# Modulation blocks queued behind feed-forward steps, and tap products and softmax division on ScalarE, in a two-block Trainium2 kernel

## The chip, the cores and the metric

The kernel runs on one core of a Trainium2 chip. The metric is device time in microseconds (us). The engines are TensorE (PE; PEld is its weight load), VectorE (DVE), ScalarE (ACT), GpSimd (POOL) and SyncE (SP), whose queue issues the DMAs. Each engine executes its instructions in the order in which the program has them; what a wait holds up, holds up all that is behind it on that engine.

## What is computed

Two transformer blocks, one behind the other, on 256 tokens of 1024 channels in fp32. The first is feed forward, mixer, feed forward, norm. The second has two layers, each a feed forward, a mixer and a feed forward, and carries a second stream, a context of 256 tokens (C, beside the tokens' X). Its norms are modulated by vectors that are computed from a condition:

```python
mod = jax.nn.silu(c) @ w_ada[l] + b_ada[l]          # 9 vectors of 1024 a layer; c_ctx likewise
sh1, sc1, gt1, sh2, sc2, gt2, sh3, sc3, gt3 = jnp.split(mod, N_ADA, axis=-1)
h = h + HALF * gt1 * swiglu_2(ada_norm(h, g_ffn1[l], sh1, sc1), w1_ffn1[l], w3_ffn1[l], w2_ffn1[l])
...
# in the mixer: convolution module, attention, Fourier branch
v = a * jax.nn.sigmoid(gt)
v = lax.conv_general_dilated(v, w_dw[:, None, :], ...)   # 31 taps on each of 384 channels
p = jax.nn.softmax(s, axis=-1)
o = jnp.einsum('bhqk,bkhd->bqhd', p, v)
```

## The kernel before

**Products.** Every fp32 product is made of three. A weight block `wr` of 512 KB is loaded, `split` casts it to a high part `wh` on ACT (L94) and subtracts that on DVE for the low part `wl` (L95); `mm3` (L110) then issues high by high, high by low and low by high. Activations are split the same way (`gH`, `gL`, `xH`, `xL`, `r`). There are 3 buffers each of `wr`, `wh` and `wl`, and in PSUM 3 of `pg` and 2 of `pm`.

**Feed forwards.** `ffn` (L210) runs over 22 blocks of 128 hidden channels in groups of 8, 7 and 7. For each block of a group comes a gating step (two weight blocks, 48 products, then `sl`, `gg` and the split of `gg`); behind a group come 8 down steps (one weight block, 24 or 21 products, and a `residual` into `h`, L292). The two feed forwards of the first block work on 256 columns (called FFN1a and FFN1b here); those of the second block work on both streams, 512 columns (a[0], b[0], a[1]), apart from the last.

**Modulation.** `ada(l, i)` (L340) computes the three vectors of one feed forward or mixer: 24 blocks, each one DMA of 512 KB into `wa` (2 buffers) and for each stream a multiply-and-sum over `wa` on DVE into `wz` (L356, 1 buffer). `ada(0,0)` runs in FFN1a, `ada(0,1)` and `ada(0,2)` are issued at a[0], `ada(1,0)` at b[0], and `ada(1,1)` and `ada(1,2)` behind it for a[1]. What orders all instructions is a scheduler: each has a priority, by the order of the code, and `spread_over` (L335) gives the blocks of `ada` priorities spread evenly over a stretch, so that they are taken when an engine has room.

**Norms and hand-over.** `norm_streams` (L295) norms a stream into `xH`, `xL`. For the first feed forward of the second block the context's norm stands ahead of FFN1b in the code; `hand_over` (L784) ends the first block and norms X. a[0] starts with three gating steps split by stream (`lead`), the context first.

**Mixers.** A `Mixer` is made for each stream and layer: mc and mx in layer 0, and mx in layer 1 (there mc gives keys and values alone). `conv_in` writes the 384 gated channels, in three tiles of 128, with padding to `vpad`. `taps` (L1158 on) sums the 31 taps of two tiles on DVE (L1164). `taps_pool` (L1149 on) does the third tile on POOL: for taps 1 to 30 a product into `tap`, 1 buffer (L1155), and an addition to the sum (L1156). Next on PE come keys (`ktc`, `ktx`), values (`vc`, `vx`), queries (`w_uq`, four blocks of 768 columns; copies to `qT`, L1074) and `attention`: scores, exp on ACT (L1101), the division by a multiply with 1/`den` on DVE (L1103), transposes (L1106) and products with the values.

## Time and profile before

| | us |
|---|---|
| median of 3 runs (2726.71 to 2731.24) | 2728.09 |
| profiled execution, its own time | 2729.1 |
| its span | 2727.3 |
| PE busy | 2622.9 (96%) |
| DVE busy | 1938.3 (71%) |
| ACT busy | 1153.4 (42%) |
| POOL busy | 334.0 (12%) |

The span is one execution on the chip as the profiler recorded it; the time of the profiled execution is 1.8 us longer than its span and 1.0 us above the median. An engine's busy time counts its own instructions. Rows of a timeline give the start in us, the duration, engine, line, operation, output and inputs; "x3" means three instructions in a row, and the brackets at the end give how long the engine stood idle before and what ended that. Matmul durations overlap, so the pace of PE is read from starts, not durations. PEclk is the clock that TensorE was granted, 1.00 for 2.4 GHz.

### The profile page before, as it was taken

Reading aid. Unit: us, or ns where it says so; the run is one execution under the profiler, and the core shown is the slowest. Engines: PE = TensorE matmul, PEld = TensorE weight load, DVE = VectorE, ACT = ScalarE, POOL = GpSimd, SP = SyncE. Lnnn points to the kernel's source line nnn. Section 1 sums busy time; section 2 is a strip of 40 time slices with the busy share of each in tenths; the row PEclk is TensorE's granted clock in tenths of the full one; section 3 lists DMA queues with packets and bytes.
Section 4 is the critical chain, followed back from the end, with each engine's and each line's share of the span. In section 5 each row is a group of like instructions: output and inputs, shape, how many; then the busy total and the mean of one; then the engine's idle time right before and its main releaser. Section 6 shows DMA issues by size and latency. Waiting matters only on the chain.

```text
span 2727.3 us, 44461 instructions
## 1 busy us (share of the span) xinstructions
PE 2622.9 (96%) x17394; PEld 2372.5 (87%) x17394; DVE 1938.3 (71%) x3490; ACT 1153.4 (42%) x1940; POOL 334.0 (12%) x354
## 2 busy tenths in 40 slices
PE   7999999998999999998999999999999999899998
PEld 7998979998788888788899878789888889799998
DVE  8988877668996359859877998736333348967666
ACT  5445535444222236654565322224222236566444
POOL 1110311110000006507300000000000002800000
PEclk9999999999999999999999999999999999999999
DMA  7774404655674234234556677733232333246564
GB/s 266 255 224 150 148 23 150 182 174 188 219 226 142 95 94 142 84 96 135 171 155 195 223 225 232 246 103 98 87 95 90 101 108 113 74 140 194 179 184 133
DMA packets 129770, 418.47 MB, mean 153 GB/s; under 512 B 18159, under 2 KB 25839, under 8 KB 129176
## 3 DMA queue, kind: packets, MB, share of 16 engines
q1 hardware_dynamic: 129160, 415.23, 48.8%
q8 instruction: 137, 2.24, 0.3%
q14 instruction: 73, 0.60, 0.1%
q10 hardware_dynamic: 400, 0.39, 0.0%
HBM read 414.24 MB, written 1.33 MB: 152 GB/s over the span
## 4 chain that ended last, share of the span: by engine, by line
PE 67%; DVE 18%; issue 7%; DMA 5%; ACT 2%; POOL 0%; DVEq 0%; SPq 0%; ACTq 0%; POOLq 0%
PE pg L113 15%; PE pg L112 15%; PE pg L114 15%; PE pm L112 6%; PE pm L113 6%; PE pm L114 6%; DVE wl L95 5%; DMA wa<-in_w_ada 4%; DVE wz L356 3%; DVE f L1164 3%; ACT wh L94 1%; PE pa L1113 1%; PE pm L1096 1%; PE pt L1106 1%; DVE un L180 1%
## 5 line engine op out<-in xcount | busy, mean ns | idle before, releaser
L94 ACT CAST wh<-wr 128x1024 fp32r<-128x1024 f32 (+3 forms) x664 | 649.8, 980 | 1108.3 <-PE pg L113 687.7
L95 DVE TENSOR_TENSOR wl<-wr,wh 128x1024 fp32r<-128x1024 f32 (+3 forms) x664 | 760.9, 1147 | 330.6 <-ACT wh L94 325.0
L114 PE MATMUL pg<-xH,wl 128*128 128x256 f32 (+2 forms) x2176 | 674.0, 310 | 7.8 <-DVE wl L95 7.8
L112 PE MATMUL pg<-xH,wh 128*128 128x256 f32 (+2 forms) x2176 | 672.4, 310 | 7.3 <-ACT wh L94 6.1
L113 PE MATMUL pg<-xL,wh 128*128 128x256 f32 (+2 forms) x2176 | 672.2, 309 | 0.5 <-DVE xL L199 0.5
L114 PEld LDWEIGHTS pg<-xH,wl 128*128 128x128 f32 x2176 | 413.4, 190 | 32.9 <-DVE wl L95 9.9
L112 PEld LDWEIGHTS pg<-xH,wh 128*128 128x128 f32 x2176 | 413.2, 190 | 31.1 <-ACT wh L94 6.1
L113 PEld LDWEIGHTS pg<-xL,wh 128*128 128x128 f32 x2176 | 413.1, 190 | 24.2 <-issue 2.2
L112 PE MATMUL pm<-xH,wh 128*128 128x256 f32 (+2 forms) x1112 | 366.4, 330 | 5.8 <-ACT wh L94 4.2
L114 PE MATMUL pm<-xH,wl 128*128 128x256 f32 (+2 forms) x1112 | 365.9, 329 | 0.8 <-DVE wl L95 0.8
L113 PE MATMUL pm<-xL,wh 128*128 128x256 f32 (+2 forms) x1112 | 366.5, 330 | 0.0
L356 DVE CUSTOM_DVE_ANT_0 wz<-wa,cb,vec 128x1024 f32<-128x1024 f32 x256 | 332.7, 1300 | 42.9 <-DMA wa<-in_w_ada 39.6
L112 PE MATMUL pg<-gH,wh 128*128 128x256 f32 (+1 forms) x972 | 325.3, 336 | 10.7 <-ACT gH L94 9.7
L113 PE MATMUL pg<-gL,wh 128*128 128x256 f32 (+1 forms) x972 | 326.0, 336 | 1.7 <-DVE gL L95 1.5
L114 PE MATMUL pg<-gH,wl 128*128 128x256 f32 (+1 forms) x972 | 324.8, 335 | 1.2 <-DVE wl L95 1.2
L112 PEld LDWEIGHTS pm<-xH,wh 128*128 128x128 f32 x1112 | 210.2, 189 | 27.2 <-ACT wh L94 4.4
L114 PEld LDWEIGHTS pm<-xH,wl 128*128 128x128 f32 x1112 | 210.3, 189 | 22.0 <-DVE wl L95 1.3
L113 PEld LDWEIGHTS pm<-xL,wh 128*128 128x128 f32 x1112 | 210.2, 189 | 20.4
L112 PEld LDWEIGHTS pg<-gH,wh 128*128 128x128 f32 x972 | 183.8, 190 | 33.1 <-ACT gH L94 11.7
L113 PEld LDWEIGHTS pg<-gL,wh 128*128 128x128 f32 x972 | 184.3, 190 | 24.3 <-DVE gL L95 3.9
L114 PEld LDWEIGHTS pg<-gH,wl 128*128 128x128 f32 x972 | 184.0, 189 | 21.9 <-DVE wl L95 1.6
L112 PE MATMUL pg<-r,wh 128*128 128x256 f32 x560 | 161.2, 288 | 8.4 <-DVE qT L1076 4.5
(408 smaller groups left out, 3658.8 us busy)
## 6 DMA issues: line engine op xcount, KB each, us to landing
wa<-in_w_ada SPq DMA_DIRECT2D x144, 512.0 KB, 4.3
wr<-in_w13a SPq DMA_DIRECT2D x88, 512.0 KB, 3.6
wr<-in_w13b SPq DMA_DIRECT2D x88, 512.0 KB, 4.1
wr<-in_w_bg SPq DMA_DIRECT2D x72, 512.0 KB, 3.5
wr<-in_w_in SPq DMA_DIRECT2D x67, 512.0 KB, 3.6
wr<-in_w_1b SPq DMA_DIRECT2D x52, 512.0 KB, 3.9
wr<-in_w_1a SPq DMA_DIRECT2D x51, 512.0 KB, 4.5
wr<-in_w_out SPq DMA_DIRECT2D x32, 512.0 KB, 4.4
```

The lines of the kernel that those rows point to most:

```text
L94: self.nc.scalar.copy(H, src)
L95: self.nc.vector.tensor_tensor(L, src, H.bitcast(F32), op=ALU.subtract)
L112: mm(ps, aH, bH, start=start, stop=False)
L113: mm(ps, aH, bL, start=False, stop=False)
L114: mm(ps, aL, bH, start=False, stop=stop)
L180: nc.vector.scalar_tensor_tensor(u, src[:, k, s], gain[:, k:k + 1], y, op0=ALU.mult, op1=ALU.mult)
L356: nc.vector.tensor_tensor_reduce(z, w, self.cb[:, s], 1.0, self.v("b_ada", l)[:, c:c + 1], ALU.mult, ALU.add, self.cols[l][:, c, s:s + 1])
L1096: mm(ss[:, n * T:(n + 1) * T], self.qT[:, h, _blk(t)], kt[:, h], start=True, stop=True)
L1106: nc.tensor.transpose(pt[:, _blk(n)], E[:, _blk(n)], net.ident)
L1113: mm(po[64 * e:64 * e + 64, _blk(t)], keys[n // 2][1][:, n % 2, 64 * h:64 * h + 64], ets[e][:, _blk(n)], start=n == 0, stop=n == nk // P - 1)
L1164: nc.vector.scalar_tensor_tensor(acc[:, j], self.pads[:, j, t:t + T], self.w31[:, j, t:t + 1], acc[:, j], op0=ALU.mult, op1=ALU.add)
```

## The change

Four things change.

1. `ada` no longer issues its blocks. It queues them, and a new `drip` takes blocks from the queue behind each of the first 38 gating and down steps of a feed forward: as many as are left, divided by the steps that are left of the 38, rounded up. Of 24 queued blocks one goes behind each of the first 24 steps, of 12 one behind each of the first 12, of 48 two behind each of the first 10 and one behind each of the next 28. Each `wz` is ordered behind the last DVE instruction of its step (`issue_after`). `spread_over` is gone.
2. `ada(0,0)` is cut in two: 12 blocks in FFN1a, 12 in FFN1b, for which the condition's rows are loaded (`ada_rows`) once more. `ada(1,1)` and `ada(1,2)` are in a[1] and no longer in b[0] as well.
3. The context's norm for a[0] stands behind FFN1b, since the blocks that it needs now end in it.
4. In the mixers the tap products go from POOL to ACT, with 2 buffers of `tap`; the additions stay on POOL. The softmax's multiply by 1/`den` goes from DVE to ACT.

```diff
     def split(self, H, L, src):
         self.nc.scalar.copy(H, src)
-        self.nc.vector.tensor_tensor(L, src, H.bitcast(F32), op=ALU.subtract)
+        return self.nc.vector.tensor_tensor(L, src, H.bitcast(F32), op=ALU.subtract)
...
+        slots = MF + 3 * KD - 8
...
+            def drip(ins):
+                nonlocal slots
+                if slots > 0:
+                    self.drip(ins, slots)
+                slots -= 1
...
-                gating(m, p)
+                drip(gating(m, p))
...
-                down(m, W, self.pg(), s)
+                drip(down(m, W, self.pg(), s))
...
-    def ada(self, l, i, pool, pace, streams=(0, 1)):
+    def ada(self, l, i, pool, streams=(0, 1), part=range(24)):
...
+        def block(j, after):
             c = 24 * i + j
-            tc.cur_priority = pace.pop(0)
             w = self.sb(pool, [P, D], "wa", 2)
             nc.sync.dma_start(w, self.A["w_ada"][l, c])
             for s in streams:
...
                 z = self.sb(pool, [P, D], "wz", 1)
+                with self.tc.issue_after(after.ins):
+                    nc.vector.tensor_tensor_reduce(z, w, self.cb[:, s], 1.0, self.v("b_ada", l)[:, c:c + 1],
+                                                   ALU.mult, ALU.add, self.cols[l][:, c, s:s + 1])
+            if j == 23:
+                self.ada_end(l, i, streams)
+
+        self.queue += [lambda after, j=j: block(j, after) for j in part]
+
+    def drip(self, ins, left):
+
+        for _ in range(-(-len(self.queue) // left)):
+            self.queue.pop(0)(ins)
...
-                    self.ada(0, 0, fp, self.spread_over(24, 150, 1500))
+                    self.ada(0, 0, fp, part=range(12))
...
-                self.norm_streams(C, m[0][0], m[0][1])
                 xn, (self.xH, self.xL) = (self.xH, self.xL), x1
                 with pool("ff") as fp:
+                    self.ada_rows(fp)
+                    self.ada(0, 0, fp, part=range(12, 24))
                     self.ffn(A["w13_1b"], A["w2_1b"], X, 0.5, r, fp=fp)
             self.xH, self.xL = xn
+            self.norm_streams(C, m[0][0], m[0][1])
...
-                p = self.spread_over(48, 350, 1400)
-                self.ada(0, 1, fp, p[:24])
-                self.ada(0, 2, fp, p[24:])
+                self.ada(0, 1, fp)
+                self.ada(0, 2, fp)
...
-                self.ada(1, 0, fp, self.spread_over(24, 150, 1200))
+                self.ada(1, 0, fp)
...
-                p = self.spread_over(48, 150, 1200)
-                self.ada(1, 1, fp, p[:24])
-                self.ada(1, 2, fp, p[24:], (0,))
+                self.ada(1, 1, fp)
+                self.ada(1, 2, fp, (0,))
...
-                    nc.vector.tensor_scalar(E, E, den, None, op0=ALU.mult)
+                    nc.scalar.activation(E, E, AF.Copy, scale=den)
...
-            z = self.sb([P, T], "tap")
-            nc.gpsimd.tensor_scalar(z, self.pads[:, 2, t:t + T], self.w31[:, 2, t:t + 1], None, op0=ALU.mult)
+            z = self.sb([P, T], "tap", 2)
+            nc.scalar.activation(z, self.pads[:, 2, t:t + T], AF.Copy, scale=self.w31[:, 2, t:t + 1])
             nc.gpsimd.tensor_tensor(acc[:, 2], acc[:, 2], z, op=ALU.add)
```

The order of instructions changes in three places that matter here. First ACT in layer 0, from the values of the context's mixer to its first exp. A name's numbers tell its buffer; 768 columns are a block of `w_uq`, 1024 columns a block of the next projection, `w_in` of mx. Before:

```order
L1062 COPY vc_1795_10526<-pg_1922_11160 128x512
L94 CAST wh_1935_11231<-wr_1934_11229 128x768
L1074 COPY qT_1923_11168<-pg_1927_11175 64x256
L94 CAST wh_1940_11261<-wr_1939_11259 128x768
L1074 COPY qT_1923_11168<-pg_1928_11187 64x256
L1074 COPY qT_1923_11168<-pg_1932_11205 64x256
L94 CAST wh_2052_11586<-wr_2051_11584 128x1024
L1074 COPY qT_1923_11168<-pg_1933_11217 64x256
L1074 COPY qT_1923_11168<-pg_1937_11235 64x256
L94 CAST wh_2056_11618<-wr_2055_11616 128x1024
```

After, the end of the same stretch (the first tap stands 31 rows ahead of the first row here; from there on two taps stand between one other instruction and the next):

```order
L1164 ACTIVATE tap_1903_11072<-vpad_1850_10800,w31_1849_10798 128x256
L94 CAST wh_1931_11204<-wr_1930_11202 128x768
L1164 ACTIVATE tap_1904_11075<-vpad_1850_10800,w31_1849_10798 128x256
L1164 ACTIVATE tap_1905_11078<-vpad_1850_10800,w31_1849_10798 128x256
L94 CAST wh_1936_11234<-wr_1935_11232 128x768
L1164 ACTIVATE tap_1906_11081<-vpad_1850_10800,w31_1849_10798 128x256
L1164 ACTIVATE tap_1907_11084<-vpad_1850_10800,w31_1849_10798 128x256
L1083 COPY qT_1924_11171<-pg_1933_11208 64x256
```

And at its end:

```order
L1164 ACTIVATE tap_1911_11096<-vpad_1850_10800,w31_1849_10798 128x256
L1083 COPY qT_1924_11171<-pg_1938_11238 64x256
L94 CAST wh_1941_11264<-wr_1940_11262 128x768
L1083 COPY qT_1924_11171<-pg_1939_11250 64x256
L1110 ACT_TABLE_LOAD
L1110 ACTIVATE f2_1951_11301,den2_1950_11298<-pm_1948_11295,mx2_1949_11297 128x256
L94 CAST wh_2053_11589<-wr_2052_11587 128x1024
```

The 30 taps now stand among the casts of `w_uq`: the second of its four casts stands behind tap 22, the third behind tap 24, the last behind tap 30, and the first cast for `w_in` moved from ahead of the exp to behind it.

Second, DVE at the first down steps of FFN1a. Before, at the last down steps of its first group:

```order
L292 SCALAR_TENSOR_TENSOR h_1_69<-pg_203_1036,h_1_69 128x256
L356 ISA wz_56_224,mod0_24_161<-wa_54_220,cb_26_163,vec_2_70 128x1024
L356 ISA mod0_24_161 128x1
L95 TENSOR_TENSOR wl_216_1131<-wr_214_1128,wh_215_1130 128x1024
L292 SCALAR_TENSOR_TENSOR h_1_69<-pg_207_1068,h_1_69 128x256
```

After:

```order
L299 SCALAR_TENSOR_TENSOR h_1_69<-pg_133_776,h_1_69 128x256
L358 ISA wz_129_768,mod0_24_161<-wa_127_764,cb_26_163,vec_2_70 128x1024
L358 ISA mod0_24_161 128x1
L95 TENSOR_TENSOR wl_146_849<-wr_144_846,wh_145_848 128x1024
L358 ISA wz_135_804,mod0_24_161<-wa_134_802,cb_26_163,vec_2_70 128x1024
L358 ISA mod0_24_161 128x1
L299 SCALAR_TENSOR_TENSOR h_1_69<-pg_140_814,h_1_69 128x256
```

Where a down step had one `wz`, each of the first four has two; behind the twelfth step there is none. FFN1b, which had none, has the same pattern.

Third, DVE in b[0], at the last gating step of its second group. Before:

```order
L356 ISA wz_3506_19608,mod1_25_162<-wa_3505_19606,cb_2984_16665,vec_2_70 128x1024
L356 ISA mod1_25_162 128x1
L356 ISA wz_3508_19612,mod1_25_162<-wa_3507_19610,cb_2984_16665,vec_2_70 128x1024
L356 ISA mod1_25_162 128x1
L247 TENSOR_TENSOR gg_3244_18244<-sl_3243_18242,pm_3242_18217 128x512
```

After:

```order
L248 TENSOR_TENSOR gg_3237_18231<-sl_3236_18229,pm_3235_18204 128x512
L95 TENSOR_TENSOR wl_3256_18314<-wr_3254_18311,wh_3255_18313 128x896
L95 TENSOR_TENSOR gL_3149_17722<-gg_3237_18231,gH_3148_17721 128x512
L358 ISA wz_3239_18237,mod1_25_162<-wa_3238_18235,cb_2985_16668,vec_2_70 128x1024
L358 ISA mod1_25_162 128x1
```

Before, `gg` stood behind two `wz`; after, the `wz` stand behind the step's `gg` and `gL`.

## Rows read from the trace of the kernel before

**Rows 1.** Stage windows: length, then PE, PEld, DVE, ACT, POOL busy (instructions), clock, DMA:

```profile
0.00:205.00 205.00, 186.41 (x1508) 183.33 (x1509) 179.86 (x283) 95.25 (x137) 30.34 (x32) 0.98 0.76 249
...
461.00:630.00 169.00, 166.67 (x1398) 165.47 (x1399) 110.35 (x161) 78.60 (x114) 26.00 (x18) 1.00 0.60 180
...
1046.00:1156.00 110.00, 100.48 (x715) 88.04 (x714) 102.06 (x223) 68.06 (x165) 74.15 (x75) 0.98 0.34 104
...
1224.00:1360.00 136.00, 120.17 (x958) 117.04 (x958) 120.99 (x198) 64.88 (x109) 74.69 (x67) 0.97 0.51 156
...
2250.00:2380.00 130.00, 117.42 (x856) 108.37 (x855) 114.85 (x247) 74.13 (x156) 70.76 (x80) 0.95 0.31 98
```

**Rows 2.** Timeline of POOL in layer 0, from the first tap:

```profile
1060.08 1.08 POOL L1155 TENSOR_SCALAR tap<-vpad,w 128x256 f32<-128x256 f32 x1
1061.24 0.74 POOL L1156 TENSOR_TENSOR f<-f,tap 128x256 f32<-128x256 f32 x1
1062.09 1.77 POOL L1155 TENSOR_SCALAR tap<-vpad,w 128x256 f32<-128x256 f32 x1
...
1075.41 1.54 POOL L1156 TENSOR_TENSOR f<-f,tap 128x256 f32<-128x256 f32 x1
```

**Rows 3.** Groups of POOL by line (count, busy us, mean ns, idle us before):

```profile
L1155 POOL TENSOR_SCALAR tap<-vpad,w 128x256 f32<-128x256 f32 x90 | 106.2, 1180 | 8.6
L1156 POOL TENSOR_TENSOR f<-f,tap 128x256 f32<-128x256 f32 x90 | 83.2, 924 | 7.5
```

**Rows 4.** Timeline of ACT in layer 0, beside those taps:

```profile
1064.53 0.83 ACT L94 CAST wh<-wr 128x768 fp32r<-128x768 f32 x1 [0.42 <-PE pg L113]
...
1081.83 0.42 ACT L132 ACTIVATE acc<-fb 128x256 f32<-128x256 f32 x1
```

**Rows 5.** Timeline of PE there, at two blocks of queries:

```profile
1068.29 0.58 PE L112 MATMUL pg<-r,wh 128*128 128x256 f32 x1 [2.62 <-DVE qT L1078]
...
1073.48 0.47 PE L112 MATMUL pg<-r,wh 128*128 128x256 f32 x1
```

**Rows 6.** Timeline of POOL in layer 1, its first tap:

```profile
2320.21 1.08 POOL L1155 TENSOR_SCALAR tap<-vpad,w 128x256 f32<-128x256 f32 x1
```

**Rows 7.** Timeline of PE in layer 1, at two blocks of queries:

```profile
2331.92 0.58 PE L112 MATMUL pg<-r,wh 128*128 128x256 f32 x1 [4.53 <-DVE qT L1076]
...
2337.59 0.28 PE L114 MATMUL pg<-r,wl 128*128 128x256 f32 x1
```

**Rows 8.** Line L1103: count, min/median/max in ns, and who waited for it:

```profile
L1103 DVE TENSOR_SCALAR f<-f,den x48: 396/488/953, 1078.5 to 2399.6; 128x512 f32<-128x512 f32 x32, 128x256 f32<-128x256 f32 x16
...
  PE pt L1106: 5.1, 13
```

**Rows 9.** Timeline of DVE in FFN1a, one down step and its modulation block:

```profile
139.38 1.09 DVE L95 TENSOR_TENSOR wl<-wr,wh 128x896 fp32r<-128x896 f32 x1
140.39 0.42 DVE L292 SCALAR_TENSOR_TENSOR h<-pg,h 128x256 f32<-128x256 f32 x1
140.72 1.28 DVE L356 CUSTOM_DVE_ANT_0 wz<-wa,cb,vec 128x1024 f32<-128x1024 f32 x1
...
141.93 1.09 DVE L95 TENSOR_TENSOR wl<-wr,wh 128x896 fp32r<-128x896 f32 x1
```

**Rows 10.** Timeline of DVE in FFN1b, two residuals of following down steps:

```profile
552.79 0.42 DVE L292 SCALAR_TENSOR_TENSOR h<-pg,h 128x256 f32<-128x256 f32 x1 [0.35 <-PE pg L114]
...
555.25 0.42 DVE L292 SCALAR_TENSOR_TENSOR h<-pg,h 128x256 f32<-128x256 f32 x1 [0.47 <-PE pg L114]
```

**Rows 11.** Timeline of PE at three of its longest waits:

```profile
137.03 0.50 PE L112 MATMUL pg<-gH,wh 128*128 128x256 f32 x2 [2.88 <-ACT gH L94]
...
656.42 0.98 PE L163 MATMUL pn<-io,hy 128*128 128x128 f32 x3 [6.76 <-DVE hy L798]
...
1725.24 0.79 PE L112 MATMUL pg<-gH,wh 128*128 128x512 f32 x1 [4.65 <-ACT gH L94]
```

**Rows 12.** Window behind the third of them (columns as in rows 1):

```profile
1723.00:1730.00 7.00, 4.60 (x10) 3.32 (x11) 5.97 (x11) 1.56 (x2) 0.00 (x0) 0.51 0.78 235
```

More of the change, by code (lines that the diff above doesn't have):

```diff
@@ L247, in gating @@
                     nc.vector.tensor_tensor(gg, sl, p[1][:, :w], op=ALU.mult)
-                self.split(gH[:, m], gL[:, m], gg)
+                return self.split(gH[:, m], gL[:, m], gg)
+            def drip(ins):
[3 more added lines that the diff above has]
+                slots -= 1
             nl = 3 if lead and gi == 0 else 0
@@ L257, in ffn @@
                 for m in range(nl):
-                    gating(m, pss[2 * m:2 * m + 2])
+                    drip(gating(m, pss[2 * m:2 * m + 2]))
             for m in range(nl, n):
@@ L271, in down @@
                              k == 0, k == n - 1)
-                self.residual(m, ps[:, rel(q)], q, gate)
+                return self.residual(m, ps[:, rel(q)], q, gate)
             nt = 4 if tail and gi == len(GROUPS) - 1 else 0
@@ L291, in residual @@
             sc = gate if isinstance(gate, float) else gate[:, m, q.start // T:q.start // T + 1]
-            self.nc.vector.scalar_tensor_tensor(self.h[:, m, q], src, sc, self.h[:, m, q],
-                                                op0=ALU.mult, op1=ALU.add)
+            r = self.nc.vector.scalar_tensor_tensor(self.h[:, m, q], src, sc, self.h[:, m, q],
+                                                    op0=ALU.mult, op1=ALU.add)
+        return r
     def norm_streams(self, s, gain, shift):
@@ L333, in ada_rows @@
         self.nc.scalar.activation(self.cb, self.cb, AF.Silu)
-    def spread_over(self, n, start, length):
-        p = self.tc.cur_priority
-        return [p + start + length * i // n for i in range(n)]
-    def ada(self, l, i, pool, pace, streams=(0, 1)):
-        nc, tc = self.nc, self.tc
-        prio = tc.cur_priority
-        for j in range(24):
+    def ada(self, l, i, pool, streams=(0, 1), part=range(24)):
+        nc = self.nc
+        def block(j, after):
             c = 24 * i + j
-            tc.cur_priority = pace.pop(0)
             w = self.sb(pool, [P, D], "wa", 2)
@@ L355, in ada @@
                 z = self.sb(pool, [P, D], "wz", 1)
-                nc.vector.tensor_tensor_reduce(z, w, self.cb[:, s], 1.0, self.v("b_ada", l)[:, c:c + 1],
-                                               ALU.mult, ALU.add, self.cols[l][:, c, s:s + 1])
-        tc.cur_priority = prio
-        self.ada_end(l, i, streams)
+                with self.tc.issue_after(after.ins):
[7 more added lines that the diff above has]
+            self.queue.pop(0)(ins)
     def ada_end(self, l, i, streams):
@@ L850, in build @@
                 with pool("ff") as fp:
-                    self.mod = [{}, {}]
+                    self.mod, self.queue = [{}, {}], []
                     self.cols = [self.sb(self.cp, [P, 72, 2], f"mod{l}") for l in range(2)]
                     self.ada_rows(fp)
-                    self.ada(0, 0, fp, self.spread_over(24, 150, 1500))
+                    self.ada(0, 0, fp, part=range(12))
                     self.ffn(A["w13_1a"], A["w2_1a"], X, 0.5, r, fp=fp, first=first)
```

## The prediction

> **What bounds the kernel now.** I read the stage table first [rows 1]: for each stretch, its length, PE's busy time, DVE's, and the clock. PE fills 166.7 of 169 us in FFN1b and 186.4 of 205 in FFN1a; what it loses, it loses in few places, above all the three mixer stretches: 110 − 100.5 = 9.5 us, 136 − 120.2 = 15.8 and 130 − 117.4 = 12.6. In these DVE is busy 102, 121 and 115 us, that is some 90% of the time: there DVE sets the pace, and POOL's 74 us (tap products and additions, [rows 3]) lie beside it. So PE is the bound nearly everywhere, and a saving on DVE or POOL counts only where PE stands idle today. Second come the single waits of PE [rows 5, 7, 11], which name what ended them. Third, the order of the instructions on ACT: ACT is busy 68 of 110 us in the first mixer stretch, so there is room for 30 more instructions, but what decides is what stands behind them.
>
> **Taps on ACT, the largest term.** Removed: 90 products on POOL, 106.2 us [rows 3]. Nobody waits for them today; the additions' result is wanted only at the end of the convolution. Added: 90 products on ACT. Such an instruction isn't in the trace; the nearest is a 128x256 ACT pass from memory to memory, 0.42 us [rows 4], and 30 of them make 12.6 us a mixer. That time isn't the price. The price is a wait: with two `tap` buffers, tap t+2 waits for addition t on POOL, and ACT goes no further until then. The 30 taps stand in the middle of the casts for `w_uq`, so the casts take the pace of POOL's additions. The last `w_uq` cast stands behind tap 30, and tap 30 behind addition 28.
>
> Pace of an addition: the shortest is 0.74 us [rows 2], from its start to the next instruction's 0.85; by the mean of 0.924 [rows 3] it is about 1.02; one that falls beside a weight split on DVE took 1.54 [rows 2]. I take 0.92, between the two, since few weight splits run in a stretch in which the casts are held. 28 additions: 25.8 us, with ends of 23.8 and 28.6.
>
> The Trainium skill, "GPSIMD Engine Reference", section Key points, says that GpSimd shares its SBUF interfaces with VectorE and contends with DVE instructions that have two SBUF inputs, which the 1.54 us addition agrees with. Its section on elementwise cycle accounting gives a two-input operation about 2.6 cycles an element at 1.2 GHz; an estimate from that page for 256 elements is 0.55 us and some fixed cost, and at 0.55 the two large mixer terms would be 28 × 0.37, some 10 us, smaller each. It makes the two-input operation the dear one, while here the one-input products' mean of 1.18 us is above the additions' 0.924 [rows 3], and the measurement decides.
>
> Layer 0, the context's mixer: the first tap starts at 1060.1 [rows 2], so tap 30 ends at 1060.1 + 0.4 + 25.8 + 0.4 = 1086.7. Behind it a copy (about 0.4, like the pass), the last `w_uq` cast (0.83, [rows 4]) and its `wl` (about 0.9, from 1.01 for 896 columns [rows 9]): its products start at about 1088.8. Today they start at 1073.48 [rows 5]. That is 15.3 us later, and PE has nothing else, since every weight block behind it (the `w_in` of the other mixer) needs a cast that stands further back on ACT. The wait of 2.62 us [rows 5] is inside this. PE comes out of so long a wait at half clock: in b[0], behind one of 4.65 us that ends at 1725.24 [rows 11], the granted clock is 0.51, the lower level of 1.2 GHz, up to about 1730 [rows 12], and 4.8 us at half speed lose 2.4. I take +2. DVE goes on with its own taps meanwhile, so the stretch behind, which has its share of the 9.5 us that PE idles [rows 1], may give back 3 to 4. Net 15.3 + 2 − 4, +13 (10 to 17).
>
> Layer 1: first tap at 2320.2 [rows 6], tap 30 ends at 2346.8, the last block's products start 2.1 us later, at 2348.9. Today they start at about 2338: PE stood still until 2331.92 for a query copy on DVE, and is through the third block at 2337.59 [rows 7]. 11 us later, +2 for the clock, −2 given back: +11 (8 to 14).
>
> Layer 0, the tokens' mixer (from 1247): the same 30 taps, but DVE is busy without a break there and casts have more slack, so ACT's delay of 2 to 7 us lies mostly beside DVE's, and POOL has left the stretch some 40 us sooner: +1 (−4 to +6).
>
> **The softmax division.** 48 multiplies leave DVE, 0.49 us each at the median [rows 8], 24 us, and come to ACT at some 0.4 to 0.6. PE waited 5.1 us for them in 13 places [rows 8]; it will now wait for ACT, behind a cast at worst: 0 (−3 to +3).
>
> **FFN1a.** A block is two `wz`; from start to start one takes 1.21 us, a `wl` of 896 columns 1.01 and a residual 0.33 [rows 9]; a `wl` of 1024 columns, in proportion, 1.15. A down step takes PE 2.46 us with 21 products [rows 10], so 2.81 with the 24 of the first group. With one `wz` a step DVE needs 1.15 + 0.33 + 1.21 = 2.69 and keeps up. With a whole block it needs 3.90, 1.09 more than PE. Four such steps: +4.4, the lower end being what the three weight buffers let DVE run ahead, some 2 us. Today's wait of 2.88 us at the end of the second group's gating [rows 11] goes, as its blocks are now in FFN1b. Gating steps are balanced: two `wl`, two `wz` and three small ones like the residual, 5.7 us, against 48 products, 5.6. I take +2 (0 to +4).
>
> **FFN1b.** It has no block today and idles 2.3 us in all [rows 1]. The same four steps cost +4.4, and at the end of the group's gating `gg` queues behind a block, as it did where PE waited 2.88 us [rows 11]; I take 1.6 of that. +6 (+3 to +9).
>
> **Hand-over.** Today 8 `wz` stand in the short chain of small instructions that makes the norm's factor, and PE waits 6.76 us [rows 11]. These go. But the context's norm, which ran inside FFN1b, now starts when FFN1b ends, and PE has no product until its factor is there: a chain of the same kind, with nothing to hide it. One such wait in place of another: 0. The nearest row gives both ends: −7 if only the old wait goes, +7 if a second one comes beside it.
>
> **a[0]**: four `wz` behind a gating step make DVE's step 2.3 + 4.8 + some 1.2 us = 8.3 against PE's 11.2 (twice the 5.6, with twice the columns), and the later down steps are as today: +0.5. **b[0]**: today `gg` stands behind two `wz`, PE waits 4.65 us [rows 11], and the half clock behind it loses 2.4 more. After, no block stands ahead of `gg` there: −7 (−8 to −4). a[1] gets blocks that DVE has room for: 0.
>
> **Sum.** +13 + 11 + 1 + 0 + 2 + 6 + 0 + 0.5 − 7 = +26.5 us on the profiled 2729.1, so 2755.6; that execution lies 1.0 above the median, so against the median 2728.1 + 26.5 = 2754.6. I put 2754.
>
> **The rivals.**
> A, faster: ACT isn't held. This decides at one number: between two pairs of taps ACT has one copy of 0.37 us and the two taps, together some 1.1 us; if an addition comes in under 0.55 us, POOL is never late. Against it: the shortest takes 0.74, and 0.85 to the next start [rows 2]. For it: POOL loses over half of its 189 us on taps [rows 3], so DVE meets it less often. Then the mixers win instead of losing: of the 37.9 us that PE idles there, I give a third to a half, −15; with FFN1a, FFN1b, a[0] and b[0] at +1.5 it ends at 2728.1 − 13.5 = 2714.6. Chance 0.13. A weaker form of it, in which the order on PE lets most of the wait be given back behind, because DVE is then far ahead (mixers +6): 2728.1 + 6 + 1.5 = 2735.6, between 2725 and 2740; chance 0.15.
>
> B, much slower: additions at 1.02 us, nothing given back, the hand-over with a second wait and FFN1b at its upper end: mixers +37 (17 + 14 + 6), the rest +1.5 + 7 + 3: 2728.1 + 48.5 = 2776.6. Chance 0.15. What would set it off is that DVE, with its backlog of own taps, keeps slowing POOL.
>
> C, the change doesn't do what it says: the scheduler could have put the blocks elsewhere. The order shows each `wz` behind its step, so I give it no chance of its own.
>
> **Numbers.** The forecast has 0.57, from 2740 to 2766; A's two forms 0.28; B 0.15. The range leaves out a part of A's first form and the tip of B: 2714 to 2778. A difference of 0.2%, 5.5 us, is about what a measurement of this kernel can tell from none. Faster by more than that is A's first form and a small part of its second: 0.16. Within it, most of the second: 0.10. Slower: 0.74.
>
> **What would show it.** Right: in the profile after, ACT's taps in layer 0 spread over some 26 us, each second one waiting for an addition on POOL; PE idle for over 10 us between 1060 and 1090 and again near layer 1's taps, ended by a `w_uq` cast or its `wl`; no wait of 4 us in b[0]; waits of about 1 us at each of the first down steps of FFN1b, ended by `wl`; a wait of some 10 us ahead of a[0]'s first products, in place of the one of 6.76. Wrong: additions under 0.6 us, or `w_uq` casts that don't wait for POOL; then the mixer stretches get shorter than 110, 136 and 130 us and the time falls below 2728. If the mixers come out as said and the time doesn't, the error lies in the feed forwards or the hand-over.

## The result and the profile after

The changed kernel took 2756.86 us, median of 4 runs (2755.08 to 2760.5), beside 2727.4 for the kernel before: 1.0111 times as long, with a 95% interval of 1.0091 to 1.013. The prediction was 2754, slower.

Its profiled execution is the longest of the four (2760.5, span 2758.7). The page's busy times say where to look: against rows 1 and the table of before, POOL lost 116 us and DVE 20, ACT gained 68, and PE's share fell.

```profile
PE 2629.9 (95%) x17394; PEld 2378.8 (86%) x17394; DVE 1918.4 (70%) x3442; ACT 1221.7 (44%) x2079; POOL 217.6 (8%) x264
```

The two traces can be laid beside each other at the products with `gH`, which every feed forward has in the same number: by how much later than in the kernel before does each stage end? The differences from one such mark to the next, in us, with the same differences for the runs below (single executions; stages that a run did not alter differ by up to 3):

| stage | predicted | after | taps alone (e2) | multiply alone (e5) | taps undone (e1) | even (e3) | late taps (e7) | even, taps undone (e8) |
|---|---|---|---|---|---|---|---|---|
| FFN1a | +2 | +2.5 | −1.0 | −2.3 | +2.8 | −9.5 | +1.9 | −8.6 |
| first block's mixer and FFN1b | +6 | +5.6 | −2.4 | −1.4 | +3.9 | −6.3 | +3.4 | −7.4 |
| hand-over to a[0]'s first down step | 0 | +4.7 | +0.6 | +1.5 | +3.0 | +5.0 | +3.1 | +4.9 |
| rest of a[0] | +0.5 | −0.6 | +0.8 | +0.2 | −0.9 | −0.6 | −0.6 | −0.9 |
| layer-0 mixers to b[0]'s first down step | +14 | +14.8 | +15.5 | −3.4 | −3.7 | +15.3 | +14.9 | −2.9 |
| b[0] | −7 | −8.1 | +1.4 | −1.4 | −7.8 | −7.8 | −7.8 | −8.1 |
| a[1] | 0 | +0.2 | −0.3 | +0.2 | 0.0 | +0.2 | −0.3 | −0.3 |
| layer-1 mixers to the last feed forward | +11 | +12.6 | +13.3 | −5.0 | −4.9 | +10.8 | +1.1 | −6.0 |

**The mixers.** ACT in layer 0 (start, duration, instruction, in brackets the idle time before and its releaser) is the stretch that answers to [rows 4]:

```profile
1071.34 0.91 ACT L1164 ACTIVATE tap<-vpad,w 128x256 f32<-128x256 f32 x2 [0.55 <-POOL vpad L1017]
...
1074.01 0.51 ACT L1164 ACTIVATE tap<-vpad,w 128x256 f32<-128x256 f32 x1 [0.36 <-POOL f L1165]
...
1086.63 0.35 ACT L1083 COPY qT<-pg 64x256 f32<-64x256 f32 x1
...
1090.09 0.81 ACT L94 CAST wh<-wr 128x768 fp32r<-128x768 f32 x1
...
1091.82 0.81 ACT L94 CAST wh<-wr 128x768 fp32r<-128x768 f32 x1
...
1099.43 0.37 ACT L1083 COPY qT<-pg 64x256 f32<-64x256 f32 x1 [5.79 <-PE pg L114]
...
1102.01 0.51 ACT L1164 ACTIVATE tap<-vpad,w 128x256 f32<-128x256 f32 x1 [0.36 <-POOL f L1165]
...
1102.81 0.83 ACT L94 CAST wh<-wr 128x768 fp32r<-128x768 f32 x1
```

POOL and DVE in the same stretch:

```profile
1072.34 22.67 POOL L1165 TENSOR_TENSOR f<-f,tap 128x256 f32<-128x256 f32 x26
```

```profile
1071.51 21.88 DVE L1173 SCALAR_TENSOR_TENSOR f<-vpad,w,f 128x256 f32<-128x256 f32 x26
1093.42 0.49 DVE L1087 TENSOR_SCALAR qT<-pg,k 64x256 f32<-64x256 f32 x1
...
1096.44 0.94 DVE L95 TENSOR_TENSOR wl<-wr,wh 128x768 fp32r<-128x768 f32 x1
```

The last tap starts at 1102.01, 31 us behind the first; the last cast for the queries follows it. 26 additions take 22.67 us, 0.87 each, and every second tap waits for one. The view by line of the additions counts ACT's waits for them in all three mixers (total us, times):

```profile
  ACT tap L1164: 15.2, 38
```

PE's longest waits there and in layer 1, in place of the 2.62 and 4.53 us of [rows 5, 7], stand ahead of the first scores; the second block of queries comes behind these:

```profile
1094.06 0.77 PE L1105 MATMUL pm<-ktc,qT 128*128 128x256 f32 x1 [8.86 <-POOL f L1165]
...
1096.58 0.78 PE L112 MATMUL pg<-r,wh 128*128 128x256 f32 x1
...
2363.63 0.77 PE L1105 MATMUL pm<-ktx,qT 128*128 128x256 f32 x1 [10.28 <-DVE qT L1085]
```

The first wait is put down to an addition, but scores read `ktc` and `qT` alone, and DVE's half of the first query copy, which starts at 1093.42, ends 0.15 us ahead of them. So both waits end with DVE's half of that copy, not with a cast. ACT's half stands behind 18 taps; DVE's stands behind tap sums, in layer 1 like this:

```profile
2354.14 0.35 ACT L1083 COPY qT<-pg 64x256 f32<-64x256 f32 x1
```

```profile
2341.68 21.34 DVE L1173 SCALAR_TENSOR_TENSOR f<-vpad,w,f 128x256 f32<-128x256 f32 x25
2363.06 0.43 DVE L1085 TENSOR_TENSOR qT<-pg,k 64x256 f32<-64x256 f32 x1
```

DVE's order changed with ACT's: 34 tap sums of the mixer stand ahead of its half in layer 0 and 40 in layer 1, where the kernel before and e1 have 19 and 26. Counted from the last product with `gH` ahead of the mixer, ACT's half comes 10.7 us later than in the kernel before in layer 0 and 10.9 in layer 1. DVE's half starts 6.4 and 8.6 us behind the end of ACT's, where it was 3.6 and 7.0. So the first query copy is 13.5 and 12.5 us late, and the two stages lose 14.8 and 12.6: most of it is ACT's hold, and 2.8 and 1.6 us are DVE's queue.

The two halves in layer 0 of the kernel before:

```profile
1063.74 0.37 ACT L1074 COPY qT<-pg 64x256 f32<-64x256 f32 x1
```

```profile
1067.74 0.49 DVE L1078 TENSOR_SCALAR qT<-pg,k 64x256 f32<-64x256 f32 x1
```

**Feed forwards and hand-over.** PE at the places of [rows 11]:

```profile
37.32 0.39 PE L112 MATMUL pg<-xH,wh 128*128 128x256 f32 x1 [1.59 <-ACT wh L94]
...
39.25 0.39 PE L114 MATMUL pg<-xH,wl 128*128 128x256 f32 x1 [1.42 <-DVE wl L95]
...
81.02 0.39 PE L114 MATMUL pg<-gH,wl 128*128 128x256 f32 x1 [0.80 <-DVE wl L95]
...
468.33 0.38 PE L112 MATMUL pm<-xH,wh 128*128 128x256 f32 x1 [2.37 <-ACT wh L94]
...
647.56 0.55 PE L163 MATMUL pn<-io,ry 128*128 128x128 f32 x1 [9.06 <-DVE ry L123]
...
651.20 0.58 PE L112 MATMUL pg<-xH,wh 128*128 128x256 f32 x1 [2.45 <-ACT xH L185]
```

The wait of 0.80 us comes at each of four down steps of FFN1a and three of FFN1b. A down step with a whole block on DVE, beside [rows 9]:

```profile
78.21 0.42 DVE L299 SCALAR_TENSOR_TENSOR h<-pg,h 128x256 f32<-128x256 f32 x1
78.54 1.27 DVE L358 CUSTOM_DVE_ANT_0 wz<-wa,cb,vec 128x1024 f32<-128x1024 f32 x1
...
79.75 1.22 DVE L95 TENSOR_TENSOR wl<-wr,wh 128x1024 fp32r<-128x1024 f32 x1
80.88 1.28 DVE L358 CUSTOM_DVE_ANT_0 wz<-wa,cb,vec 128x1024 f32<-128x1024 f32 x1
...
82.09 0.42 DVE L299 SCALAR_TENSOR_TENSOR h<-pg,h 128x256 f32<-128x256 f32 x1
```

From residual to residual 82.09 − 78.21 = 3.88 us, where PE needs 2.81: DVE sets the pace of these steps, as the sum of 3.90 had it. The window in b[0] that answers to [rows 12] is full and at full clock:

```profile
1740.00:1760.00 20.00, 20.00 (x88) 16.07 (x87) 13.00 (x21) 4.40 (x5) 0.00 (x0) 1.00 0.46 144
```

### The profile page after: what moved, and what is told of

Its sections match the earlier page's. It is cut to its first block, busy times and chain, and to the rows that moved or that the text cites. A ratio compares the mean times of both kernels' runs of the same rounds, so it can differ in the third digit from the quotient of the medians.

```text
span 2758.7 us, 44505 instructions
## 1 busy us (share of the span) xinstructions
PE 2629.9 (95%) x17394; PEld 2378.8 (86%) x17394; DVE 1918.4 (70%) x3442; ACT 1221.7 (44%) x2079; POOL 217.6 (8%) x264
## 4 chain that ended last, share of the span: by engine, by line
PE 75%; DVE 10%; issue 3%; ACT 2%; DMA 1%; POOL 0%; DVEq 0%; ACTq 0%; POOLq 0%; SPq 0%
PE pg L112 16%; PE pg L113 16%; PE pg L114 16%; PE pm L112 6%; PE pm L113 6%; PE pm L114 6%; DVE f L1173 3%; DVE wl L95 2%; PE pm L1105 1%; PE pa L1122 1%; ACT wh L94 1%; DVE wz L358 1%; PE pt L1115 1%; PE pn L163 0%; DMA wr<-in_w_1b 0%
## 5 line engine op out<-in xcount | busy, mean ns | idle before, releaser
L248 DVE TENSOR_TENSOR gg<-sl,pm 128x512 f32<-128x512 f32 (+1 forms) x107 | 61.8, 577 | 207.0 <-PE pm L114 185.8
```

What stands on the lines that cost most here:

```text
L248: nc.vector.tensor_tensor(gg, sl, p[1][:, :w], op=ALU.mult)
```

## The experiments

They ran in three groups, each on a chip of its own and beside the kernel before, whose median was 2729.3 us for e1 to e4, 2727.4 for e5 to e8 and 2728.1 for e9 to e12.

**e1, taps undone.**

```diff
-            z = self.sb([P, T], "tap", 2)
-            nc.scalar.activation(z, self.pads[:, 2, t:t + T], AF.Copy, scale=self.w31[:, 2, t:t + 1])
+            z = self.sb([P, T], "tap")
+            nc.gpsimd.tensor_scalar(z, self.pads[:, 2, t:t + T], self.w31[:, 2, t:t + 1], None, op0=ALU.mult)
```

> The changed kernel with one part undone: the tap products are on GpSimd again with one buffer; the softmax multiply stays on ScalarE and the modulation blocks stay queued. First theory (ScalarE is held at the pace of GpSimd's additions, and so are the casts behind): the two mixer stretches that lost 14.8 and 12.6 us against the kernel before get these back, 2757 - 27 = 2730 us, between 2725 and 2736. Rival (it is the softmax multiply on ScalarE, or the modulation blocks, that make the mixers late): it stays above 2745.

2721.71 us, 0.9975 of before (0.9963 to 0.9986). The theory holds, and the size was too small: 35 us came back, not 27. The mixers are now 3.7 and 4.9 us shorter than before, which the multiply alone can have made (e5).

**e2, taps alone.** The kernel before with this alone:

```diff
-            z = self.sb([P, T], "tap")
-            nc.gpsimd.tensor_scalar(z, self.pads[:, 2, t:t + T], self.w31[:, 2, t:t + 1], None, op0=ALU.mult)
+            z = self.sb([P, T], "tap", 2)
+            nc.scalar.activation(z, self.pads[:, 2, t:t + T], AF.Copy, scale=self.w31[:, 2, t:t + 1])
```

> The kernel before with one part of the change alone: the tap products on ScalarE with two buffers. First theory: the hold needs nothing else of the change, so the time is that of before plus 25 to 27 us, 2753 us, between 2747 and 2760, with PE idle for some 9 us ahead of the first scores in layer 0 and for some 10 us in layer 1. Rival (the taps cost little by themselves, the loss needs the softmax multiply on ScalarE too): below 2740.

2757.29 us, 1.0096 (1.008 to 1.0113): 28 us for this part alone, all of it in the two mixer stretches. The new order on DVE, with 34 and 40 tap sums ahead of the first query copies, comes with this part. The rival, that the loss needs the multiply too, falls.

**e5, multiply alone.** The kernel before with one line:

```diff
-                    nc.vector.tensor_scalar(E, E, den, None, op0=ALU.mult)
+                    nc.scalar.activation(E, E, AF.Copy, scale=den)
```

> The kernel before with one part alone: the softmax multiply on ScalarE instead of VectorE. Theory formed from the run with the taps back on GpSimd, whose mixer stretches were 3.8 and 4.9 us shorter than before: VectorE sets the pace of the mixers, 24 us of it go, and some 8 us come out: 8 us under before, between 4 and 11 under. Rival, the one of the prediction (the multiply moves from one engine that PE waits for to another): the time of before, within 3 us.

2720.68 us, 0.9973 (0.9963 to 0.9983): 7 us faster, as its theory had it; the table shows 3.4 and 5.0 us in the mixers. On ACT the 48 multiplies cost more than they did on DVE: 31.4 us, 654 ns each,

```profile
L1103 ACT ACTIVATE f<-f,den 128x512 f32<-128x512 f32 (+1 forms) x48 | 31.4, 654 | 12.7 <-DVE den L1102 12.5
```

against 0.488 us at the median in [rows 8]. The kernel gains all the same, since DVE is the engine whose instructions the others queue for there; its tap sums of the context's mixer end at 1119.8 us instead of 1134.3, and 2 us of that are from the stages ahead. In the changed kernel the multiply's gain is hidden behind the hold: against e2, which has the taps alone, the two mixer stretches are only 0.7 us shorter each. So the taps cost 35 us beside it (e1 against the changed kernel), 28 without it (e2).

**e6, additions left out.** The additions of taps 1 to 28 are gone, so the third convolution tile isn't the sum of its taps; all products are there.

```diff
-            nc.gpsimd.tensor_tensor(acc[:, 2], acc[:, 2], z, op=ALU.add)
+            if t > 28:
+                nc.gpsimd.tensor_tensor(acc[:, 2], acc[:, 2], z, op=ALU.add)
```

> The changed kernel with the additions of taps 1 to 28 on GpSimd left out (the third convolution tile is then not the sum of its taps); all 30 products on ScalarE remain and wait for nobody. First theory (the price is ScalarE's wait for the additions): what is left is a block of 30 products, some 13 to 15 us on ScalarE ahead of the casts, about half of the hold, and VectorE's own tap sums no longer meet GpSimd's additions and drop from 0.84 to some 0.5 us each; 2757 - 18 = 2739 us, between 2731 and 2746. Rival (the price is ScalarE's time for 90 products): they are all still there, 2752 or more.

2729.46 us, 1.0011 (1.0001 to 1.002): 27 us less than the changed kernel with all its 90 products, where 18 were expected and 5 or less by the rival. So the rival falls, and most of the price is not ACT's time for the products. But that time isn't free. ACT now runs them in one piece, 0.40 us apart, and PE waits for what stands behind:

```profile
1073.21 12.08 ACT L1164 ACTIVATE tap<-vpad,w 128x256 f32<-128x256 f32 x30 [0.55 <-POOL vpad L1017]
```

```profile
1086.11 0.79 PE L112 MATMUL pg<-wh,r 128*128 128x512 f32 x1 [12.39 <-ACT ktc L1064]
```

In layer 1 the like wait is 12.16 us, and the run is 8 us above e1, where POOL has the products. The run also takes away two things at once, ACT's wait for additions and the additions that DVE's tap sums meet. These sums (count, min/median/max in ns) are near their minimum throughout, 89.2 us in all instead of 118.5 in the changed kernel and 112.6 in the kernel before, which may be why I expected too little; no run parts the two:

```profile
L1174 DVE SCALAR_TENSOR_TENSOR f<-vpad,w,f x180: 468/473/959, 1059.8 to 2346.2; 128x256 f32<-128x256 f32 x180
```

**e9 and e10, DVE's tap sums left out.** Of the 60 sums in each mixer 56 are gone, so two convolution tiles aren't the sums of their taps: e9 with the products on ACT, e10 with the products on POOL.

```diff
-            for t in range(1, 31):
+            for t in range(1, 3):
                 nc.vector.scalar_tensor_tensor(acc[:, j], self.pads[:, j, t:t + T], self.w31[:, j, t:t + 1], acc[:, j],
```

> The changed kernel with 56 of VectorE's 60 tap sums left out in each mixer (two convolution tiles are then not the sums of their taps); ScalarE's products and GpSimd's additions are all there. To be read against the next run, in which the products are on GpSimd. First theory (the hold is ScalarE waiting for additions, and nothing else is needed): the difference between the two stays what it was with VectorE's sums, 35 us or little less, with additions still some 0.85 us apart. Second theory (part of the hold is VectorE: the splits of the query weights stand behind 26 tap sums that run at 0.84 us beside the additions): the difference shrinks to between 15 and 27 us.

> The same 56 of VectorE's 60 tap sums left out in each mixer, with the tap products on GpSimd as in the kernel before; softmax multiply on ScalarE and queued blocks as in the changed kernel. VectorE then sets the pace of no mixer stretch: 2722 - 15 = 2707 us, between 2697 and 2715. Rival (the mixers' idle time comes from the chains of norms and softmax, not from VectorE's load): 2717 or more.

2738.12 us (1.0033, 1.0021 to 1.0045) and 2690.45 us (0.9861, 0.9846 to 0.9875). The difference is 48 us, not smaller than 35 but larger. So the second theory's number falls: ACT's hold costs PE time with DVE's queue nearly empty. What grew is layer 0: by the marks of the table the runs differ by 30.7 us there and 15.6 in layer 1, where the changed kernel and e1 differ by 18.5 and 17.5. That with DVE free nothing else is late, so that the hold costs more, is a reading and not a test. In layer 0 DVE now stands idle for 15 us, waiting for ACT, while POOL's additions come 10.41/13 = 0.80 us apart and ACT waits for them as before:

```profile
1081.39 0.49 DVE L1087 TENSOR_SCALAR qT<-pg,k 64x256 f32<-64x256 f32 x1 [15.10 <-ACT qT L1083]
```

```profile
1067.63 10.41 POOL L1165 TENSOR_TENSOR f<-f,tap 128x256 f32<-128x256 f32 x13
```

```profile
1072.43 0.51 ACT L1164 ACTIVATE tap<-vpad,w 128x256 f32<-128x256 f32 x1 [0.30 <-POOL f L1165]
```

The 30 additions of this stretch take 25.5 us, against 31.4 in the changed kernel. So DVE's tap sums do lengthen the stretch, by 6 us, as the second theory had it. ACT's half of the first query copy of layer 0 comes 9.9 us later than in e10, and it came 10.8 later in the changed kernel than in e1, so the hold is there with DVE's sums and without them. DVE's half now follows ACT's at once, and PE's waits for it in the two layers are short, where they were 8.86 and 10.28 us:

```profile
1082.03 0.77 PE L1105 MATMUL pm<-ktc,qT 128*128 128x256 f32 x1 [1.43 <-DVE qT L1087]
...
2338.82 0.45 PE L1105 MATMUL pm<-ktx,qT 128*128 128x256 f32 x1 [2.14 <-DVE qT L1085]
```

The products on ACT with the old order on DVE were not run. e10's own expectation was missed on the fast side: 31 us less than e1, not 15.

**e7, taps later in the order.** The calls that issue products and additions stand behind the attention (and, in layer 0, the other mixer's latents).

```diff
                 mc.conv_in()
-                mc.taps_pool()
                 mc.keys()
                 mc.queries()
                 mc.attention()
                 mx.latents()
+                mc.taps_pool()
...
-                mx.taps_pool()
                 mx.keys()
                 mx.queries()
                 mx.attention()
+                mx.taps_pool()
                 mx.fourier()
```

> The changed kernel with the call that makes GpSimd's third of the convolution moved behind the attention (context's mixer of layer 0, mixer of layer 1), so that the 60 tap products of these two stand among ScalarE's softmax work and no longer among the casts for the queries. First theory (what counts is what stands behind the held taps): between two taps ScalarE now has more work than an addition takes, so it is hardly held, and the two stretches get back 25 us or more: 2757 - 27 = 2730 us, between 2722 and 2740. Rival (wherever taps wait for additions, ScalarE's order holds PE as long): 2750 or more.

2748.73 us, 1.0076 (1.0061 to 1.0091), between the two. In layer 1 the stretch loses 1.1 us instead of 12.6, as the theory has it. In layer 0 it loses 14.9 as before, but elsewhere: the context's attention, reckoned from the end of a[0], now starts 6 us earlier than in the kernel before, and the time goes behind it, where taps stand among the casts for the other mixer and meet DVE's tap sums:

```profile
1129.32 0.58 PE L163 MATMUL pn<-io,ry 128*128 128x128 f32 x1 [3.02 <-DVE ry L123]
...
1138.90 0.58 PE L112 MATMUL pg<-xH,wh 128*128 128x256 f32 x1 [3.52 <-ACT wh L94]
...
1142.48 0.58 PE L114 MATMUL pg<-xH,wl 128*128 128x256 f32 x1 [2.78 <-DVE wl L95]
```

**e3, blocks spread evenly** over the 38 steps (12 blocks: one behind every third).

```diff
-        for _ in range(-(-len(self.queue) // left)):
+        self.slot += 1
+        for _ in range(self.slot * self.queued // self.slots - (self.slot - 1) * self.queued // self.slots):
             self.queue.pop(0)(ins)
```

> The changed kernel with its modulation blocks spread evenly over the 38 steps, 12 blocks one behind every third step, instead of one behind each of the first 12. First theory (where two multiply-and-sums stand behind each step VectorE needs more time than PE): the first feed forward loses some 3 us less and the second some 7 us less, 2757 - 9 = 2748 us, between 2744 and 2752, and the waits of 0.8 us at the down steps of the first group go. Rival (the second feed forward loses by the reload of the condition's rows and by the transfers that share the DMA engines): no block less is loaded, so 2755 or more.

2736.5 us, 1.0026 (1.0016 to 1.0036): 20 us less than the changed kernel, where 9 were expected. In the table, which goes by single executions, FFN1a gains 12.0 us on the changed kernel and the stage with FFN1b 11.9; no wait above 0.7 us is left in either but the two at the start. The rival falls as it was put: the condition's rows are still loaded twice, and FFN1b is none the slower. But the even spread thins out the blocks' transfers as well as their work on DVE. The waits of 0.80 us at the down steps are DVE's by the rows; the one of 2.37 us in FFN1b ended with a cast that itself had waited 1.82 us for its block's transfer, and no run parts the two there.

**e12, the whole first third in FFN1a**, 24 blocks spread evenly over 38 steps, taps on POOL, and the context's norm ahead of FFN1b as in the kernel before. Beside the lines of e1 and e3:

```diff
-                    self.ada(0, 0, fp, part=range(12))
+                    self.ada(0, 0, fp)
...
+                self.norm_streams(C, m[0][0], m[0][1])
                 xn, (self.xH, self.xL) = (self.xH, self.xL), x1
                 with pool("ff") as fp:
-                    self.ada_rows(fp)
-                    self.ada(0, 0, fp, part=range(12, 24))
...
-            self.norm_streams(C, m[0][0], m[0][1])
```

> As the run that took 2701 us (even spread, products on GpSimd, multiply on ScalarE), but all 24 blocks of the first third are in the first feed forward, 24 behind 38 steps, and the context's norm stands ahead of the second feed forward as in the kernel before. Theory (one block behind two of three steps still leaves single down steps short of VectorE time; the hand-over gets its norm for nothing): the first feed forward loses 6 us, the second gains 0, the hand-over gains 8: 2699 us, between 2694 and 2705. Rival (halving the blocks is what made the gain): 2707 or more.

2713.83 us, 0.9943 (0.993 to 0.9956), 12.5 us more than e8, which differs in this alone: the rival is right. FFN1a ends 10.4 us later than in the kernel before, with waits such as

```profile
68.66 0.39 PE L112 MATMUL pg<-gH,wh 128*128 128x256 f32 x1 [2.36 <-ACT gH L94]
...
205.62 0.39 PE L112 MATMUL pg<-gH,wh 128*128 128x256 f32 x1 [2.02 <-ACT gH L94]
```

Pinned behind its step, a block costs more than at the place that the scheduler gave it; only with few blocks a step does the pinning cost nothing. The hand-over did gain, 6 us in its stage where 8 were expected.

**e4, the context's norm inside FFN1b**, queued behind the last block.

```diff
+                def ctx_norm(after):
+                    self.xH, self.xL = xn
+                    self.norm_streams(C, m[0][0], m[0][1])
+                    self.xH, self.xL = x1
...
+                    self.queue.append(ctx_norm)
...
-            self.norm_streams(C, m[0][0], m[0][1])
```

> The changed kernel with the context's norm emitted behind the last modulation block of the second feed forward, inside it, instead of behind the feed forward. First theory (the chain of the context's norm is what PE waits for at the hand-over, 9.1 and 2.5 us): these waits go, 3 us come back inside the feed forward as in the kernel before, 2757 - 8 = 2749 us, between 2746 and 2752. Rival (the chain of the tokens' norm is as long and ends last anyway): PE waits as long for it, 2755 or more.

2754.39 us, 1.0088 (1.0071 to 1.0105): 2.5 us less than the changed kernel, between the two expectations and no more than single runs of either differ by. The waits of 9.06 and 2.45 us are gone, and the hand-over is 11.0 us shorter than in the changed kernel, but the stage with FFN1b is 7.2 longer: behind the dense blocks the norm costs PE 2.72 us at one down step alone. At the hand-over a wait of the same size, for the tokens' norm, is left:

```profile
509.76 0.38 PE L112 MATMUL pg<-gH,wh 128*128 128x256 f32 x1 [2.72 <-ACT wh L94]
...
661.14 0.35 PE L143 MATMUL pn<-io,un 128*128 128x1 f32 x2 [2.72 <-DVE un L136]
```

**e8 and e11, the parts that gain.** e8 joins e1 and e3 (even spread, products on POOL, multiply on ACT); e11 adds the norm of e4; their lines are those of the diffs above.

> The changed kernel with two parts altered: modulation blocks spread evenly over the 38 steps, and tap products back on GpSimd; the softmax multiply stays on ScalarE. If the gains of the two single runs (20 us for the even spread, 35 for the taps) lie in different stages they add up: 2757 - 55 = 2702 us, between 2697 and 2707, some 1% under the kernel before. Rival (they overlap, for instance through the clock or through waits that take each other's place): 2710 or more.

> Even spread and tap products on GpSimd, as in the run that took 2701 us, and the context's norm emitted inside the second feed forward behind the last block. If the two waits of PE at the hand-over, 8.8 and 2.2 us, can be hidden there, as they were only in part when the blocks were dense: 2701 - 6 = 2695 us, between 2691 and 2698. Rival (the norm's work costs the feed forward's last steps as much as the hand-over gains): 2699 or more.

2701.28 us (0.9907, 0.9891 to 0.9924) and 2695.77 us (0.9874, 0.986 to 0.9888). The gains add up, and behind sparse blocks the norm brings 5.5 us. At the hand-over e11 has, in place of 6.76 us in [rows 11] and of 9.06 after:

```profile
625.60 0.24 PE L143 MATMUL pn<-io,acc 128*128 128x1 f32 x1 [2.01 <-DVE acc L136]
...
639.53 0.35 PE L163 MATMUL pn<-io,hy 128*128 128x128 f32 x1 [0.92 <-DVE hy L809]
```

e11 is 32 us under the kernel before and 61 under the changed one.

## Why the prediction was right

**The taps: mechanism right, the place of it wrong, the size too small.** ACT ran at the pace of the additions, the casts for the queries stood behind, and PE came late by it: e2 and e9 show that. The pace was put at 0.92 us, by ends of 0.85 and 1.02, and was 0.87. But PE's idle time was to end with a `w_uq` cast or its `wl`, and its longest waits ended with DVE's half of the first query copy: PE has the first scores ahead of the second block of queries, which the sum left out. From this came a loop. PE issued the second block's products behind the scores, from 1096.58 on; ACT waited 5.79 us for the first of them to copy, with the last four taps behind it; and the stretch took 31 us, not 26.6. DVE was late as well, with 15 tap sums more ahead of that copy, at 0.84 us each; it split the casts at 1090.09 and 1091.82 only at 1096.44 and 1098.10. So the last block's products, put 15.3 us later, came 18.0 later (1103.69, by the same mark), of which some 3 came back within the stage, as the sum had it. "That time isn't the price", said of the taps' own 12.6 us, is not shown: with hardly an addition to wait for, PE still waits 12.39 us behind them (e6). The term "+13 + 11 + 1" measured 28 alone, and 35 beside the multiply.

**The multiply: the step that failed.** "0 (−3 to +3)", because PE would only wait for another engine; it was −7 (e5). The row of [rows 8] was read for who waits for the multiply, and not for what queues behind it on an engine that rows 1 had named as the pace of the mixers. The two errors nearly cancel: 25 predicted for mixers and multiply together, 14.8 + 12.6 = 27.4 measured. That the sum came out within 3 us of the time is luck to that extent; that the change is slower, and that the taps make it so, is not.

**FFN1a: right by its number, not by its parts.** +2 predicted, +2.5 measured. The four down steps cost what the sum said a step costs, 3.88 us on DVE, but 0.8 us of waiting each and not 1.09, and the kernel before had waits in that group as well: the group's down steps came out only 0.2 us longer. The gating steps, which were called balanced, cost 6.2 us: the blocks of the first two steps stand together on DVE, four `wz` with nothing but small instructions between them, and PE waits 1.59 and 1.42 us:

```profile
31.13 1.27 DVE L358 CUSTOM_DVE_ANT_0 wz<-wa,cb,vec 128x1024 f32<-128x1024 f32 x1
...
35.75 1.27 DVE L358 CUSTOM_DVE_ANT_0 wz<-wa,cb,vec 128x1024 f32<-128x1024 f32 x1
```

The wait at the end of the second group went (−3.1).

**FFN1b.** +6 predicted. The table has +5.6, made of +8.7 up to the last group's down steps and −3.1 behind them, where the context's norm had stood. The gating steps were missed here too.

**Hand-over.** 0 predicted, with one wait in place of another: the wait of 6.76 us went and one of 9.06 came, and 2.45 behind it; the stage lost 4.7 us, of which the 3.1 that FFN1b gained have to be taken off, since they are the same norm's; 1.6 are left against the 0 predicted. Of the 9.06 us, 2.47 are a split of weights (`xl`) that waited for its cast and that for its load, in the middle of the chain on DVE:

```profile
645.12 1.23 DVE L95 TENSOR_TENSOR xl<-wr,xh 128x1024 fp32r<-128x1024 f32 x1 [2.47 <-ACT xh L94]
646.27 0.15 DVE L122 SCALAR_TENSOR_TENSOR ra<-ra,rv 128x2 f32<-128x2 f32 x1
```

**b[0] and a[0].** −7 and +0.5 predicted, −8.1 and −0.6 measured; the wait of 4.65 us and its half clock are gone.

**The rivals.** A needed additions under 0.55 us apart; the shortest stretch, with DVE idle, had 0.80. Its weaker form, a loss given back behind because DVE is then far ahead, fails too: DVE was ahead, by 15 tap sums at its first query copy, but had come to that copy late by them, and of the 18.0 us in layer 0 only some 3 came back. B's pace of 1.02 us didn't come.

Left open: what the products would cost with the old order on DVE, how much of e6's gain is the missing contention, and why the context's mixer in e7 loses as much behind its attention as it had ahead of it, in parts; the rows show three engines waiting in turn, and no run separates them.

## What to carry to other kernels

A product moved to an engine with time to spare costs what stands behind it in that engine's order: look for the wait that the moved instruction brings (here a buffer that a slow consumer frees), and price it by the consumer's pace times the instructions ahead of the first one that the bound engine needs. Which one that is, the bound engine's own order tells: here it was the first query copy, behind 18 taps, and not the last cast, behind 30. Then read the new order on the other engines too: on DVE 15 more tap sums came to stand ahead of that copy. Work that is pinned behind a step must fit into the shortest step, not the mean one: spread over three steps a block cost nothing, one behind each step cost PE 0.8 to 2.4 us at a time. And on an engine that sets the pace of a stage, count what queues behind an operation as well as who waits for its result.

## What the runs showed of the hardware

A tap sum on DVE and an addition on POOL, each with two inputs from memory, slow each other almost into lockstep: 26 sums took 21.88 us and 26 additions 22.67 in the same stretch, 0.84 and 0.87 each. Without additions 37 sums in a row took 14.87 us, 0.40 each (e6); without sums the additions come 0.80 us apart (e9). So in this pair it is DVE that pays. I had counted this contention against the additions alone. The row of e6:

```profile
1073.38 14.87 DVE L1174 SCALAR_TENSOR_TENSOR f<-vpad,w,f 128x256 f32<-128x256 f32 x37
```

The Trainium skill, "GPSIMD Engine Reference", section Key points, names the contention for DVE instructions with two SBUF inputs; these runs agree and show its size on either side.
